# Column sums of a hybrid trunk in two fp32r passes, and low-rank products padded to 128 rows

## The chip, the cores and the metric

One core of one Trainium2 chip runs the whole kernel as one launch. The metric is the device time of that launch in microseconds (us), the median of several runs.

## The reference, cut to what matters

The network is a two-layer trunk on a stream of T = 528 positions (16 meta tokens and 512 inputs) of width 1024. Each layer has a combined input projection, four token mixers (RWKV-7, SSD, retention, RG-LRU), gated merging, an output projection and a SwiGLU block. The change touches sums over channels and the low-rank products of the RWKV mixer:

```
w_log = -softplus(-(w0 + tanh(wd) @ w2)) - 0.5      # rank 64
a = sigmoid(a0 + ad @ a2)                           # rank 64
v = v + (v_first - v) * sigmoid(v0 + (v @ v1) @ v2) # rank 32, second layer only
kk = kk / max(sqrt(sum(kk * kk, head)), 1e-12)      # sum over the 64 channels of a head
var = mean((y - mean)^2, head)
bonus = sum(r * k * r_k, head) * v
y = y * rsqrt(mean(y * y, head) + eps)              # retention, 128 channels
yg = yg * rsqrt(mean(yg * yg, group) + 1e-5)        # SSD, 256 channels
```

## The kernel before

Every activation lies with its channels on the 128 partitions and its 528 positions along the free dimension, as tiles of 128 x 528. A large projection (`dense`, L224 to L238) multiplies eight 128 x 128 weight blocks with eight activation tiles. Weights and activations are split into a high part, rounded to fp32r, and a low part, which is the rest, and three of the four products are taken (high-high, low-high, high-low), each in two halves of 264 columns: 48 matmul instructions on line L236 for one output tile. In the last layer part of the work has 512 columns and then a product is one instruction. The weight split costs one ScalarE copy (L213) and one VectorE subtraction (L214) for each group of eight blocks.

Small products are taken in plain fp32 by `halves` (L258 to L267): for each half of 264 columns it takes a PSUM bank, multiplies, and hands the bank to a function that evicts it. The hardware runs one fp32 product as two matmul instructions, so that the profile counts two for each half. `halves` serves sums over partitions, with a constant matrix as the left side: `ones` (all 128 channels) or `hb` (two blocks of 64 channels). It also serves the low-rank products, whose left side in `sw` and right side (`wdad`, `t32`) use 64 or 32 rows alone: rows 0 to 63 of `wdad` hold the decay's input, rows 64 to 127 that of the in-context rate.

The RWKV mixer works channel block by channel block (8 for each layer). `rwkv_front` (L720) computes keys, decays and the bonus: low-rank products at L736 and L751, the key norm at L756 to L762 (tile `rtmp`), the bonus sum at L790 and L809 (`rtmp` again), and in the second layer the value product at L802 (right side `t32`, called `t` in the profile). `rwkv_inverse` (L813) inverts small triangular blocks, `rwkv_back` (L892) runs the sequential chunks (32 x 32 products at L912 and L918, then a chain over L931, L936 and L947, then the outputs at L964 and L966, squared into `wy` at L975), and `rwkv_finish` (L978) takes the variance sum over `wy` (L981), normalises and multiplies with the gate product `sg` (L986). Retention takes its sum over `rxs` at L479, SSD over two tiles `M` at L654.

What runs between those chains is `others` (L1028): the other three mixers and the merge gates, handed out by `fill` in `layer` in portions of estimated work. The final order of instructions on each engine is not the order of the code: a scheduler sets it when the kernel is built, from its own estimates of durations and from priorities. `soon` raises the priority of evictions. Every engine then runs its own list strictly in order, and waits at an instruction whose input isn't there.

## Time and profile before

| | |
|---|---|
| median of 3 runs | 3588.73 us (3580.23 to 3598.2) |
| the profiled execution's own time | 3595.58 us |
| its span, first to last instruction | 3593.7 us |
| TensorE (PE) busy | 3501.6 us, 97% of the span |
| VectorE (DVE) busy | 2348.2 us, 65% |
| ScalarE (ACT) busy | 1515.9 us, 42% |
| GpSimd (POOL) busy | 175.7 us, 5% |
| mean granted TensorE clock | 0.98 |

PE is the engine for matmuls, PEld its weight loads, which overlap them. Matmuls are pipelined: the duration of one holds its way through the array, and the next one starts long before it ends. What a matmul costs in a full stream is therefore the distance from one end to the next, and not its duration. In a timeline, rows of the same kind that follow one another are merged: the row has the start of the first, the time from there to the end of the last, and their count, so that start plus time is the end of the last. A form such as 64*128 64x264 is a weight tile of 64 rows by 128 columns and a moving tile of 64 rows by 264 columns.

### The profile page before, as it was taken

What the parts mean: (1) busy time and instruction counts of PE and PEld (TensorE: products, weight loads), DVE (VectorE), ACT (ScalarE), POOL (GpSimd) and SP (SyncE); (2) the same over time, 40 slices, a digit from 0 to 9 for tenths busy, and PEclk for the clock granted to TensorE, in tenths of its full rate; (3) what the DMA queues carried; (4) which work ended last, traced back from release to release, by engine and by line L of the source; (5) the groups of instructions that cost most, each with busy time, mean ns of one, the idle gap of its engine ahead of it and who ended that gap; (6) DMA issues with size and microseconds to landing.
All of it is one profiled execution on the core that took longest, in us unless ns stands there. A gap on an engine that the chain in (4) does not pass through costs nothing.

```text
span 3593.7 us, 61305 instructions
## 1 busy us (share of the span) xinstructions
PE 3501.6 (97%) x24768; PEld 3157.5 (88%) x24768; DVE 2348.2 (65%) x4548; ACT 1515.9 (42%) x2208; POOL 175.7 (5%) x474
## 2 busy tenths in 40 slices
PE   8999999999999999999999999899999999999998
PEld 7999889899898999999988888788888887788887
DVE  7787776676787555544347788667668875555543
ACT  6555444434435324222236556344444453332222
POOL 1000100100000000000000000000000000000001
PEclk9999999999999999999999999899999999999999
DMA  3233222222224553233333333222222335533332
GB/s 126 92 100 105 84 81 87 75 83 79 75 87 130 157 171 114 89 94 93 119 103 107 92 97 93 80 87 82 85 77 73 95 117 161 174 116 96 97 95 88
DMA packets 171452, 364.39 MB, mean 101 GB/s; under 512 B 54848, under 2 KB 63424, under 8 KB 171168
## 3 DMA queue, kind: packets, MB, share of 16 engines
q1 hardware_dynamic: 169936, 359.04, 33.0%
q8 instruction: 196, 3.21, 0.4%
q10 hardware_dynamic: 1152, 1.05, 0.1%
q14 instruction: 88, 0.72, 0.1%
q0 software_dynamic: 80, 0.37, 0.0%
HBM read 308.35 MB, written 47.71 MB: 99 GB/s over the span
## 4 chain that ended last, share of the span: by engine, by line
PE 82%; DVE 8%; ACT 6%; DMA 2%; issue 2%; POOL 0%; SPq 0%; DVEq 0%; ACTq 0%; POOLq 0%
PE d L236 63%; PE s L265 4%; PE s L829 2%; PE s L931 1%; DVE wlo L214 1%; PE s L936 1%; PE s L471 1%; PE s L947 1%; PE s L639 1%; PE s L473 1%; ACT whi L213 1%; PE s L395 1%; PE s L632 1%; PE s L918 1%; PE s L912 1%
## 5 line engine op out<-in xcount | busy, mean ns | idle before, releaser
L236 PE MATMUL d<-hh,whi 128*128 128x264 f32 (+1 forms) x4928 | 1196.9, 310 | 18.8 <-ACT whi L213 9.5
L236 PE MATMUL d<-hh,wlo 128*128 128x264 f32 (+1 forms) x4928 | 1188.3, 308 | 0.0
L236 PE MATMUL d<-hl,whi 128*128 128x264 f32 (+1 forms) x4928 | 1187.3, 308 | 0.7 <-DVE hl L255 0.7
L213 ACT ACTIVATE whi<-raw 128x1024 fp32r<-128x1024 f32 (+1 forms) x462 | 485.5, 1051 | 1174.1 <-PE d L236 918.1
L236 PEld LDWEIGHTS d<-hh,whi 128*128 128x128 f32 x4928 | 809.1, 192 | 67.0 <-ACT whi L213 11.2
L236 PEld LDWEIGHTS d<-hl,whi 128*128 128x128 f32 x4928 | 804.6, 191 | 41.8 <-issue 6.4
L236 PEld LDWEIGHTS d<-hh,wlo 128*128 128x128 f32 x4928 | 806.8, 191 | 34.1 <-issue 1.7
L214 DVE TENSOR_TENSOR wlo<-raw,whi 128x1024 fp32r<-128x1024 f32 (+1 forms) x462 | 559.8, 1212 | 342.6 <-ACT whi L213 325.1
L236 PE MATMUL d<-yh,whi 128*128 128x264 f32 (+1 forms) x768 | 206.5, 325 | 4.5 <-ACT yh L254 4.5
L236 PE MATMUL d<-yh,wlo 128*128 128x264 f32 (+1 forms) x768 | 208.1, 324 | 0.0
L236 PE MATMUL d<-yl,whi 128*128 128x264 f32 (+1 forms) x768 | 208.0, 325 | 0.1
L881 DVE TENSOR_TENSOR NS<-NS,sm 36x31 f32<-36x31 f32 (+15 forms) x496 | 164.3, 331 | 11.4
L879 DVE TENSOR_TENSOR sm<-E,NS 36x31 f32<-36x31 f32 (+15 forms) x496 | 164.1, 331 | 11.4 <-DMA E<-xd 0.4
L236 PEld LDWEIGHTS d<-yh,whi 128*128 128x128 f32 x768 | 127.2, 189 | 18.7 <-ACT yh L254 7.9
L236 PEld LDWEIGHTS d<-yl,whi 128*128 128x128 f32 x768 | 128.4, 189 | 12.5 <-DVE yl L255 1.3
L236 PEld LDWEIGHTS d<-yh,wlo 128*128 128x128 f32 x768 | 128.3, 189 | 11.5
L236 PE MATMUL d<-fh,whi 128*128 128x264 f32 (+1 forms) x506 | 132.4, 318 | 0.0
L236 PE MATMUL d<-fl,whi 128*128 128x264 f32 (+1 forms) x506 | 132.0, 317 | 0.0
L236 PE MATMUL d<-fh,wlo 128*128 128x264 f32 (+1 forms) x506 | 131.6, 317 | 0.0
L1141 DVE TENSOR_TENSOR fg<-d,nr 128x528 f32<-128x528 f32 (+1 forms) x44 | 30.8, 700 | 125.7 <-PE d L236 122.4
L1024 DVE SCALAR_TENSOR_TENSOR gth<-gth,d 128x528 f32<-128x528 f32 (+1 forms) x48 | 33.4, 696 | 100.2 <-PE d L236 100.1
L1146 DVE TENSOR_TENSOR fth<-d,fth 128x528 f32<-128x528 f32 (+1 forms) x44 | 30.8, 700 | 92.3 <-PE d L236 92.2
(579 smaller groups left out, 4719.1 us busy)
## 6 DMA issues: line engine op xcount, KB each, us to landing
raw<-w SPq DMA_DIRECT2D x462, 512.0 KB
g<-gth SPq DMA_DIRECT2D x32, 264.0 KB
Bs<-acd SPq DMA_DIRECT2D x32, 264.0 KB
gth<-g SPq DMA_DIRECT2D x32, 264.0 KB
g<-gth SPq DMA_DIRECT2D x32, 256.0 KB
gth<-g SPq DMA_DIRECT2D x32, 256.0 KB
yd<-lt SPq DMA_DIRECT2D x16, 264.0 KB
ya<-wy SPq DMA_DIRECT2D x16, 264.0 KB
```

Source lines behind the costliest of these rows:

```text
L213: nc.scalar.activation(hi[:, :n], raw[:, :n], AF.Copy)
L214: nc.vector.tensor_tensor(out=lo[:, :n], in0=raw[:, :n], in1=hi[:, :n].bitcast(F32), op=SUB)
L236: nc.tensor.matmul(ps[:, h], w[:, k - k0], xv[:, h], start=(k == 0 and w is hi and xi == 0), stop=(k == nk - 1 and w is lo))
L265: self.nc.tensor.matmul(ps, lhsT, rhs[:, o:o + w], start=(i == 0), stop=(i == len(pairs) - 1))
L395: nc.tensor.transpose(ps[:, c * k:c * k + k], src[:, o:o + CL], self.c("ident")[:k, :k])
L471: fs = [lambda: nc.tensor.matmul(o, vTs[e][:, c], scs[e][:, cs], start=(c == 0), stop=True)]
L473: fs.insert(0, lambda: nc.tensor.matmul(o, R[hr, c], qr[hr, cs], start=True, stop=False))
L632: nc.tensor.matmul(ps[:, (c - 3 * a) * CL:(c - 3 * a + 1) * CL], S[:, c, e * 128:e * 128 + 128], Cs[:, c * CL:(c + 1) * CL], start=True, s ...
L639: nc.tensor.matmul(ps[i * 64:i * 64 + 64, (c - 3 * a) * CL:(c - 3 * a + 1) * CL], xdt[:, c, 2 * e + i], Ms[i][:, c * CL:(c + 1) * CL], sta ...
L829: nc.tensor.matmul(ps[:, c - c0], bk[:, c].rearrange("p s x -> p (s x)"), AR[:, c], start=True, stop=True)
L879: nc.vector.tensor_tensor(out=pr, in0=X3[:, :a, a:a + 1].broadcast_to([nl, a, w]), in1=N3[:, a:a + 1, a:].broadcast_to([nl, a, w]), op=MUL)
L881: nc.vector.tensor_tensor(out=N3[:, :a, a:], in0=N3[:, :a, a:], in1=pr, op=ADD)
```

## The change

Sums over partitions go through a new function `sums` in place of `halves`. It copies the input to an fp32r tile `hi` on ScalarE, subtracts that from the input on VectorE into an fp32r tile `lo`, and for each half multiplies both with the constant matrix in fp32r and accumulates them. The constants are loaded once more, as fp32r, into a tile `cr` (index 0 is `ones`, 1 is `hb`), with two transfers issued by GpSimd at the start. `hb` moves to the end of the constants. Four places use it: retention, SSD (two inputs), the key norm and the bonus of RWKV, and its variance. Room for `hi` and `lo` comes from tiles that are not in use there (`v`, `r`, `kkn`, `NS`, `kT`, `rv`, `kr`, `qr`, `z0`, `x0` and so on), which carry their old names in the profile. The tiles `G` and `PS_` of the chunk chain go from two buffers to one. The final norms (`norm_end`, `finish`) and the gate product keep `halves` in fp32.

The low-rank matrices are laid out on the host with zeros: `sw` has three matrices of 128 rows in place of two, the decay's with zeros in rows 64 to 127, the rate's with zeros in rows 0 to 63, and the value's with zeros from row 32. The right sides are then the whole `wdad`, and a `t32` of 128 rows that GpSimd sets to zero once. The transfer of `sw` grows from 128 x 256 to 128 x 384 numbers for each of the 16 channel blocks.

```diff
@@ -122,6 +122,10 @@
         nc.gpsimd.dma_start(out=self.cst, in_=self.io["cst"][:, :NCST0])
+        self.cr = self.t(self.cp, [2, 128], "cr", dt=F32R)
+        for i, name in enumerate(("ones", "hb")):
+            nc.gpsimd.dma_start(out=self.cr[:, i], in_=self.io["cst"][:, COFF[name]:COFF[name] + 128])
         self.kb = self.t(self.cp, 8, "kb")
@@ -265,6 +269,22 @@
                 use(ps, slice(o, o + w))
+    def sums(self, pool, const, xs, use):
+        nc = self.nc
+        parts = []
+        for x, hi, lo in xs:
+            nc.scalar.activation(hi, x, AF.Copy)
+            nc.vector.tensor_tensor(out=lo, in0=x, in1=hi.bitcast(F32), op=SUB)
+            parts += [hi, lo]
+        for o in (0, H2):
+            ps = self.bank(pool)[:, :H2]
+            for i, part in enumerate(parts):
+                nc.tensor.matmul(ps, self.cr[:, const], part[:, o:o + H2], start=(i == 0), stop=(i == len(parts) - 1))
+            with self.soon():
+                use(ps, slice(o, o + H2))
@@ -476,7 +495,9 @@
                     nc.vector.tensor_tensor(out=y[:, ts], in0=ps, in1=gs[e][:, ts], op=MUL)
-            self.halves(self.psm, [(self.c("ones"), sq)], lambda ps, ts: nc.scalar.activation(
+            room = [self.t(p, T, tag, dt=F32R) for tag in ("kr", "qr")] if e else [
+                self.t(p, [NC, 128], "kT", dt=F32R).rearrange("p c x -> p (c x)")[:, :T], self.t(p, T, "rv", bufs=2, dt=F32R)]
+            self.sums(self.psm, 0, [(sq, *room)], lambda ps, ts: nc.scalar.activation(
                 sq[:, ts], ps, AF.Ln, bias=self.bias[1e-6], scale=1.0 / 128))
@@ -649,9 +670,9 @@
             nc.scalar.activation(sq, ys[e], AF.Square)
-            sqs.append((self.c("ones"), sq))
+            sqs.append((sq, self.t(p, T, f"z{e}", dt=F32R), self.t(p, T + 3, f"x{e}", dt=F32R)[:, :T]))
         rs = self.t(p, T, "M", bufs=3)
-        self.halves(self.psm, sqs, lambda ps, ts: nc.scalar.activation(
+        self.sums(self.psm, 0, sqs, lambda ps, ts: nc.scalar.activation(
             rs[:, ts], ps, AF.Ln, bias=self.bias[1e-5], scale=1.0 / 1024))
@@ -713,19 +734,21 @@
                                  stop=(j == NT - 1))
-        self.t32 = self.t(p, T, "t32", bufs=1, parts=32)
+        self.t32 = self.t(p, T, "t32", bufs=1)
+        nc.gpsimd.memset(self.t32, 0.0)
         for h in range(2):
-            nc.scalar.activation(self.t32[:, h * H2:(h + 1) * H2], acc[h], AF.Copy)
+            nc.scalar.activation(self.t32[:32, h * H2:(h + 1) * H2], acc[h], AF.Copy)
     def rwkv_front(self, l, j, p, q):
         nc = self.nc
         m = self.psm
         src = ("w_in", l)
         V = slice(PAD, TP)
-        sw = self.t(p, [2, 128], "sw")
-        nc.sync.dma_start(out=sw, in_=self.io["rsw"][l, j, :, :2])
+        sw = self.t(p, [3, 128], "sw")
+        nc.sync.dma_start(out=sw, in_=self.io["rsw"][l, j, :, :3])
         g2 = self.t(p, 128, "g2", bufs=2)
-        nc.sync.dma_start(out=g2, in_=self.io["rsw"][l, j, :, 2])
+        nc.sync.dma_start(out=g2, in_=self.io["rsw"][l, j, :, 3])
         k = self.shift(self.dense(src, RWKV0 + 1024 + j * 128, self.X), p, "k", 8 + j, PAD)
@@ -748,16 +771,16 @@
         tha = self.t(p, T, "tha")
-        self.halves(m, [(sw[64:128, 0], self.wdad[64:128])], lambda ps, ts: nc.scalar.activation(
+        self.halves(m, [(sw[:, 1], self.wdad)], lambda ps, ts: nc.scalar.activation(
             tha[:, ts], ps, AF.Tanh, bias=self.der("na0", j), scale=-0.5))
         kk = self.t(p, TP, "kkn")
         nc.scalar.activation(kk, k, AF.Copy, scale=self.par("kk", j))
         tmp = self.t(p, T, "rtmp")
         nc.scalar.activation(tmp, kk[:, V], AF.Square)
-        n2 = self.t(p, TP + 1, "r")[:, :T]
-        self.halves(m, [(self.c("hb"), tmp)], lambda ps, ts: nc.vector.tensor_scalar(
-            out=n2[:, ts], in0=ps, scalar1=1e-24, scalar2=None, op0=MAX))
-        nc.scalar.activation(tmp, n2, AF.Ln)
+        room = [self.t(p, TP + 1, tag, dt=F32R)[:, :T] for tag in ("v", "r")]
+        self.sums(m, 1, [(tmp, *room)], lambda ps, ts: nc.vector.tensor_scalar(
+            out=tmp[:, ts], in0=ps, scalar1=1e-24, scalar2=None, op0=MAX))
+        nc.scalar.activation(tmp, tmp, AF.Ln)
         nc.scalar.activation(tmp, tmp, AF.Exp, scale=-0.5)
@@ -799,14 +822,15 @@
             thv = tha
-            self.halves(m, [(sw[0:32, 1], self.t32)], lambda ps, ts: nc.scalar.activation(
+            self.halves(m, [(sw[:, 2], self.t32)], lambda ps, ts: nc.scalar.activation(
                 thv[:, ts], ps, AF.Tanh, bias=self.der("hv0", j), scale=0.5))
             nc.vector.tensor_tensor(out=vd, in0=vd, in1=v[:, V], op=SUB)
             nc.vector.scalar_tensor_tensor(out=vd, in0=thv, scalar=1.0, in1=vd, op0=ADD, op1=MUL)
             nc.vector.scalar_tensor_tensor(out=v[:, V], in0=vd, scalar=0.5, in1=v[:, V], op0=MUL, op1=ADD)
         bv = self.t(q, T, "bv", bufs=2)
         vv = v[:, V]
-        self.halves(m, [(self.c("hb"), tmp)], lambda ps, ts: nc.vector.scalar_tensor_tensor(
+        room = [self.t(p, TP + 1, "r", dt=F32R)[:, :T], self.t(p, TP, "kkn", dt=F32R)[:, :T]]
+        self.sums(m, 1, [(tmp, *room)], lambda ps, ts: nc.vector.scalar_tensor_tensor(
             out=bv[:, ts], in0=ps, scalar=0.5, in1=vv[:, ts], op0=MUL, op1=MUL))
@@ -929,7 +953,7 @@
             nc.tensor.matmul(ps, flat(AR[:, c, 1:3]), flat(SV[:, c]), start=True, stop=True)
-            G = self.t(q, 128, "G", bufs=2)
+            G = self.t(q, 128, "G")
             with self.soon():
@@ -941,7 +965,7 @@
             if c:
-                PS_ = self.t(q, 128, "PS_", bufs=2)
+                PS_ = self.t(q, 128, "PS_")
                 nc.scalar.activation(PS_, flat(SV[:, c]), AF.Copy, scale=Pc)
@@ -975,10 +999,12 @@
-    def rwkv_finish(self, j, back):
+    def rwkv_finish(self, j, back, q):
         nc = self.nc
         y, y2, bv, g2 = back
-        self.halves(self.psr, [(self.c("hb"), y2)], lambda ps, ts: nc.scalar.activation(
+        x = self.t(q, 2 * TP, "NS", dt=F32R)
+        room = x[:, :T], x[:, T:2 * T]
+        self.sums(self.psr, 1, [(y2, *room)], lambda ps, ts: nc.scalar.activation(
             y2[:, ts], ps, AF.Ln, bias=self.bias[64e-5], scale=1.0 / 64))
@@ -1280,11 +1306,11 @@
     s0 = np.concatenate([a["meta"], a["x"][0]], axis=0).T.reshape(NT, 128, T)
-    rsw = np.zeros((DEPTH, NT, 128, 3, 128), np.float32)
+    rsw = np.zeros((DEPTH, NT, 128, 4, 128), np.float32)
     rsw[:, :, :64, 0] = a["rwkv_w2"].reshape(DEPTH, 64, NT, 128).transpose(0, 2, 1, 3)
-    rsw[:, :, 64:, 0] = a["rwkv_a2"].reshape(DEPTH, 64, NT, 128).transpose(0, 2, 1, 3)
-    rsw[:, :, :, 2] = a["rwkv_g2"].reshape(DEPTH, 128, NT, 128).transpose(0, 2, 1, 3)
-    rsw[1:, :, :32, 1] = a["rwkv_v2"].reshape(DEPTH - 1, 32, NT, 128).transpose(0, 2, 1, 3)
+    rsw[:, :, 64:, 1] = a["rwkv_a2"].reshape(DEPTH, 64, NT, 128).transpose(0, 2, 1, 3)
+    rsw[:, :, :, 3] = a["rwkv_g2"].reshape(DEPTH, 128, NT, 128).transpose(0, 2, 1, 3)
+    rsw[1:, :, :32, 2] = a["rwkv_v2"].reshape(DEPTH - 1, 32, NT, 128).transpose(0, 2, 1, 3)
     arrays = {
```

What the change does to the order is seen at three places. In the lists below, rows are PE's or ScalarE's instructions in the order in which the engine runs them; a row with x2 stands for two, and a plain fp32 product is one row though it runs as two instructions.

The first is PE at the end of channel block 0 of layer 0, where `rwkv_finish` takes the variance. Before (`wy` is the squared output, `cst` the constants, `sg` the gate's input):

```order
L236 MATMUL d<-hl,whi 128x264 x2
L236 MATMUL d<-hh,wlo 128x264 x2
L236 MATMUL d<-hh,whi 128x264
L265 MATMUL s<-wy_1495,cst 128x264
L265 MATMUL s<-sg,g_354 128x264
L236 MATMUL d<-hh,whi 128x264
L236 MATMUL d<-hl,whi 128x264 x2
```

After (`NS` holds both halves, `cr` the fp32r constants; L240 is the old L236, L285 the passes of `sums`):

```order
L240 MATMUL d<-hh,whi 128x264
L285 MATMUL s<-NS,cr 128x264 x2
L240 MATMUL d<-hh,whi 128x264
L240 MATMUL d<-hl,whi 128x264 x2
L240 MATMUL d<-hh,wlo 128x264 x2
L240 MATMUL d<-hh,whi 128x264 x2
L240 MATMUL d<-hl,whi 128x264
L285 MATMUL s<-NS,cr 128x264 x2
L240 MATMUL d<-hl,whi 128x264
L240 MATMUL d<-hh,wlo 128x264 x2
```

Before, the second half of the sum stood right ahead of the gate product; now both halves stand a few dense passes apart, each as two fp32r passes, and the gate product follows seven rows behind the last one shown.

The second is PE in channel block 2 of layer 0, where the front of block 3 meets the 32 x 32 products of the back of block 2. Before:

```order
L265 MATMUL s<-wdad,sw 128x264
L912 MATMUL s<-sm,XK 32x32 x9
L918 MATMUL s<-NS,sm 32x32 x9
L265 MATMUL s<-wdad,sw 128x264
L931 MATMUL s<-SV,AR 128x128
L265 MATMUL s<-rtmp,cst 128x264
L918 MATMUL s<-NS,sm 32x32 x9
```

After (L936 and L942 are the old L912 and L918; `v` and `r` are the high and low part of `rtmp`):

```order
L285 MATMUL s<-v,cr 128x264 x2
L240 MATMUL d<-hh,wlo 128x264 x2
L240 MATMUL d<-hh,whi 128x264
L285 MATMUL s<-r,cr 128x264 x2
L240 MATMUL d<-hh,whi 128x264
L936 MATMUL s<-sm,XK 32x32 x9
L240 MATMUL d<-hl,whi 128x264 x2
```

The low-rank products no longer stand among the 32 x 32 products, but as a pair twelve rows ahead of this piece, and the passes of the key norm come ahead of them.

The third is ScalarE in the front of channel block 2 of layer 0, between the low-rank products and the key norm. Before:

```order
L736 ACTIVATE lam<-s,pard 128x264 x2
L754 ACTIVATE kkn<-k,par 128x576
L751 ACTIVATE tha<-s,pard 128x264
L756 ACTIVATE rtmp<-kkn 128x528
L751 ACTIVATE tha<-s,pard 128x264
L760 ACT_TABLE_LOAD
L760 ACTIVATE rtmp<-r 128x528
```

After (L779 is the old L756, L768 and L771 are the old L745 and L748; L279 is the copy to `hi`):

```order
L774 ACTIVATE tha<-s,pard 128x264 x2
L768 ACTIVATE E<-ech 128x9x64
L779 ACTIVATE rtmp<-kkn 128x528
L771 ACTIVATE ech<-ech,kb 128x576
L279 ACTIVATE v<-rtmp 128x528
L217 ACTIVATE whi<-raw 128x1024
```

Two exponentials that stood behind the key norm now stand ahead of its new copy.

## Rows read from the trace of the kernel before

**Rows 1.** Page: span, busy time of each engine, chain that ended last.
```profile
span 3593.7 us, 61305 instructions
PE 3501.6 (97%) x24768; PEld 3157.5 (88%) x24768; DVE 2348.2 (65%) x4548; ACT 1515.9 (42%) x2208; POOL 175.7 (5%) x474
...
PE 82%; DVE 8%; ACT 6%; DMA 2%; issue 2%; POOL 0%; SPq 0%; DVEq 0%; ACTq 0%; POOLq 0%
PE d L236 63%; PE s L265 4%; PE s L829 2%; PE s L931 1%; DVE wlo L214 1%; PE s L936 1%; PE s L471 1%; PE s L947 1%; PE s L639 1%; PE s L473 1%; ACT whi L213 1%; PE s L395 1%; PE s L632 1%; PE s L918 1%; PE s L912 1%
```

**Rows 2.** PE by form: shapes xcount | busy us, mean ns | idle before, releasers.
```profile
L236 PE MATMUL d<-hh,whi 128*128 128x264 f32 x4256 | 923.1, 294 | 18.8 <-ACT whi L213 9.5 <-DVE Cs L313 3.1 <-DVE r L678 2.1
...
L265 PE MATMUL s<-rtmp,cst 128*128 128x264 f32 x128 | 42.5, 436 | 1.7 <-ACT rtmp L756 1.5
L265 PE MATMUL s<-wdad,sw 64*128 64x264 f32 x128 | 41.2, 434 | 0.7 <-ACT lam L736 0.7
...
L265 PE MATMUL s<-rxs,cst 128*128 128x264 f32 x64 | 22.1, 454 | 0.1
L265 PE MATMUL s<-wy,cst 128*128 128x264 f32 x64 | 21.8, 422 | 5.7 <-ACT wy L975 5.2
...
L265 PE MATMUL s<-M,cst 128*128 128x264 f32 x64 | 18.3, 409 | 0.0
...
L265 PE MATMUL s<-t,sw 32*128 32x264 f32 x32 | 9.7, 414 | 0.0
```

**Rows 3.** Timeline of PE around a key norm: start us, us, instructions.
```profile
2086.97 0.41 PE L236 MATMUL d<-hh,whi 128*128 128x264 f32 x2
2087.21 1.05 PE L265 MATMUL s<-rtmp,cst 128*128 128x264 f32 x4
2087.91 0.60 PE L236 MATMUL d<-hl,whi 128*128 128x264 f32 x2
```

**Rows 4.** The same around a low-rank product of 64 rows.
```profile
2080.52 0.40 PE L236 MATMUL d<-hh,wlo 128*128 128x264 f32 x2
2080.86 1.15 PE L265 MATMUL s<-wdad,sw 64*128 64x264 f32 x4
2081.94 0.51 PE L236 MATMUL d<-hh,whi 128*128 128x264 f32 x2
...
2084.69 1.15 PE L265 MATMUL s<-wdad,sw 64*128 64x264 f32 x4
```

**Rows 5.** ScalarE and VectorE by form: the split of a 128 x 528 tile.
```profile
L254 ACT ACTIVATE yh<-yraw 128x528 fp32r<-128x528 f32 x32 | 20.6, 644 | 16.0 <-DMA yraw<-ya 6.6 <-DMA yraw<-yb 4.7 <-DMA yraw<-yc 4.0
...
L255 DVE TENSOR_TENSOR yl<-yraw,yh 128x528 fp32r<-128x528 f32 x32 | 21.5, 703 | 13.5 <-ACT yh L254 13.4
```

**Rows 6.** Line L265: whom PE waited for (us, times).
```profile
its engine sat idle before it (us, times) until:
  ACT wy L975: 14.6, 20
  ACT wy L981: 9.7, 12
...
  ACT rtmp L756: 3.8, 5
```

**Rows 7.** Timeline of a variance sum: ScalarE and the second half on PE.
```profile
412.93 0.62 ACT L975 ACTIVATE wy<-s 64x256 f32<-64x256 f32 x2 [0.49 <-DVE wy L974]
...
414.14 1.28 ACT L981 ACT_TABLE_LOAD   x1
415.44 0.48 ACT L981 ACTIVATE wy<-s,kb 128x264 f32<-128x264 f32 x1
415.94 0.22 ACT L975 ACTIVATE wy<-s 64x64 f32<-64x64 f32 x1
...
416.22 0.71 PE L265 MATMUL s<-wy,cst 128*128 128x264 f32 x2
```

**Rows 8.** Two stretches by window: busy us of each engine, PEclk, DMA share.
```profile
639.00:646.00 7.00, 7.00 (x41) 6.29 (x41) 3.00 (x7) 1.89 (x5) 0.00 (x0) 0.51 0.21 78
902.00:909.00 7.00, 7.00 (x40) 6.08 (x40) 3.63 (x9) 3.42 (x7) 0.34 (x2) 0.52 0.17 68
```

More of the change, by code (lines that the diff above doesn't have):

```diff
@@ L43 @@
     NPAR += _c
-CCOLS = [("ident", 128), ("ones", 128), ("hb", 128), ("cent", 128), ("tri", 128), ("cau", 88),
-         ("qdec", 4 * 88), ("kdec", 4 * 88), ("cdec", 4), ("cos", T), ("sin", T)]
+CCOLS = [("ident", 128), ("ones", 128), ("cent", 128), ("tri", 128), ("cau", 88),
+         ("qdec", 4 * 88), ("kdec", 4 * 88), ("cdec", 4), ("cos", T), ("sin", T), ("hb", 128)]
 COFF, NCST = {}, 0
@@ L56 @@
 GK = 2, 3, 3
-NCST0 = COFF["qdec"]
+NCST0, NCST1 = COFF["qdec"], COFF["hb"]
 def _constants():
@@ L360, in ret_consts @@
     def ret_consts(self, p):
-        n = NCST - NCST0
-        self.rc = self.t(p, n, "rc", bufs=1)
-        self.nc.sync.dma_start(out=self.rc, in_=self.io["cst"][:, NCST0:])
+        self.rc = self.t(p, NCST1 - NCST0, "rc", bufs=1)
+        self.nc.sync.dma_start(out=self.rc, in_=self.io["cst"][:, NCST0:NCST1])
     def rcc(self, name, rows=slice(0, 128)):
@@ L735, in rwkv_front @@
         lv = lam[:, V]
-        self.halves(m, [(sw[0:64, 0], self.wdad[0:64])], lambda ps, ts: nc.scalar.activation(
+        self.halves(m, [(sw[:, 0], self.wdad)], lambda ps, ts: nc.scalar.activation(
             lv[:, ts], ps, AF.Tanh, bias=self.der("hw0", j), scale=0.5))
@@ L1097, in layer @@
                 bk = self.rwkv_back(l, j, fr, iv, p, q)
-                YA.append(self.spill("ya", j, self.rwkv_finish(j, bk)))
+                YA.append(self.spill("ya", j, self.rwkv_finish(j, bk, q)))
                 if j + 1 < NT:
```

## The prediction, made before the changed kernel was run

> **What bounds the kernel now.** I read the page first. PE is busy 97% of a span of 3593.7 us, and the chain that ended last runs over PE for 82%, 63% of it through the dense products of L236 [rows 1]. DVE at 65% and ACT at 42% have room. So the time is, to first order, what PE's list costs when it is run without holes: whatever shortens a PE instruction shortens the kernel, and work added to ACT or DVE costs something where PE's next instruction waits for it. The next view is PE by form [rows 2]. The sums of this change are 128 + 64 + 64 + 64 = 320 instructions, thus 160 fp32 products of 264 columns, and the low-rank products are 128 + 32 instructions, thus 80 products. Their mean durations (409 to 454 ns) say little, since matmuls overlap; what counts is the step from end to end, which I read from the timeline.
>
> The chosen stretch has dense pairs on both sides and no idle time [rows 3]. The dense pair ahead ends at 2086.97 + 0.41 = 2087.38, the four instructions of the key norm at 2087.21 + 1.05 = 2088.26, the next dense pair at 2087.91 + 0.60 = 2088.51. Two fp32 products took 0.88 us, **0.44 each**; two dense fp32r passes took **0.25**. There is no extra step between the two kinds. Around a 64-row product [rows 4] the same reading gives 2080.92, then 2082.01, then 2082.45: the same two products' worth of columns took 1.09 in place of 0.88, and the dense pair behind took 0.44 in place of 0.25. The product is not slower for its columns; the step into the 64-row form and out of it costs 0.21 + 0.19 = **0.40 us a block**, 0.20 a switch.
>
> **The change part by part.**
>
> Sums in fp32r: each of the 160 products becomes two fp32r passes of 264 columns. I price them by the dense pair, because shape, type and a fresh weight load for each pass are the same: 160 x (0.44 - 0.25) = **30.4 us less** on PE. Nearly all of it is on the path, as PE is.
>
> Padding: the low-rank products keep their column count and lose the form of their own. The lists of PE before and after, counted for a change of the rows or columns that neighbouring instructions use, have 607 and 513 such changes. The 94 that go are just the two ends of 47 blocks (37 of `wdad`, 10 of `t`) in the list before. 94 x 0.20 = **18.8 us less**. The 32-row blocks of `t` are priced as the 64-row ones, since their mean duration is alike (414 and 434 ns) [rows 2]. The new zero rows cost nothing on PE: the full-row product costs 0.44.
>
> One rule speaks against padding. In the rows, the decay's and the rate's products of a channel block stand 3.8 us apart with dense passes between [rows 4], so nothing of one runs beside the other. The Trainium skill, "TensorE: Matmul & The Clock Gate", section "Why this matters for your kernels", says that products of few rows that lie in distinct row groups run concurrently, so padding would give that up; by it, 16 pairs of blocks could overlap, and 16 x 0.88 = 14 us of room would be lost. The two blocks aren't neighbours in PE's list before, so the sum takes nothing for it.
>
> The new step ahead of each sum: a copy on ACT (0.644 us) and a subtraction on DVE (0.703) for a 128 x 528 tile [rows 5], 80 of each. That is 52 us for ACT and 56 for DVE, which go to about 44% and 68%. As load it lies beside PE; as latency it puts 1.35 us ahead of 72 sums (16 key norms, 16 bonuses, 16 variances, 16 in retention, 8 in SSD). What that costs depends on how far the scheduler moved the sums back in PE's list. I counted PE's rows between the last instruction that feeds a sum and the sum, at prices of the trace. Variance: median 0.85 us before, 2.8 after, so 1.9 gained against 1.35. Here the rows hold a possible gain too. PE waited 14.6 us for `wy` and 9.7 for the bank that L981 frees [rows 6], and the second half came late because a table load and the first half's logarithm (1.28 + 0.48) ran ahead of the last square [rows 7]; with the copy reading the whole tile they can't come between. I take 0, between 24 less and 16 x 1.35 = 22 more. Bonus: the passes stand 13 or more dense passes later (1.6 us) in 14 of 16 blocks, so 0. Retention: the first half can't start before the second half's square now, but the median distance grows from 1.7 to 2.9, so 0 to 2. SSD: 0, at most 8 x 1.35 = 11. Key norm: the distance grows by only 0.7 of the 1.35, and in some blocks one or two exponentials stand ahead of the copy on ACT; 16 x 0.65 = 10, of which I let 2 vanish in slack (PE waited just 3.8 there) [rows 6]. The value for all is **8 us more**, with ends at 24 less and 72 x 1.35 = 97 more; I stay near the lower end because the order shows the sums moved by more than their new step in three of five kinds.
>
> What hangs on the moved instructions: behind a waiting sum stand the dense passes, and PE can't pass it. On ACT the copy delays the next weight copy `whi` by 0.64, on DVE the subtraction delays `wlo` by 0.70; both run a group ahead of PE. Behind the variance's wait stands the gate product, which used to wait for a bank in any case.
>
> The rest I cost at nothing. Two transfers for `cr` and a memset for `t32` go to GpSimd, at 5% busy [rows 1], long before their first use. The queue of `sw` carries 64 KB more for each of 16 blocks, issued a block ahead. `G` and `PS_` with one buffer: their next writer depends, through the chain, on their last reader anyway. The list of ACT has 174 table loads in place of 190, 16 x 1.28 = 20 us of ACT, off the path. If GpSimd's transfers were late, the first key norm (at some 37 us) would wait a few us, once.
>
> Sum: -30.4 - 18.8 + 8 = -41.2. The profiled execution took 3595.58 us, so 3554.4; it lies 6.9 above the median of the runs (3588.73), so on the median's scale **3548 us**, 1.1% less.
>
> **The rivals.**
>
> *The new step becomes the wait.* PE stands at each sum until ACT and DVE have split its input. For it: the order of ACT shows exponentials and `whi` copies ahead of the new copy in places, and PE's waits at L265 for ACT show that the scheduler already placed these sums too early [rows 6]. Against: it pushed them back this time. The gains of 49.2 us are used up at 0.68 us a sum over 72 sums. Over 0.93 us a sum it is slower by more than 0.5%; all 97 give 3589 - 49 + 97 = 3637. Between 0.43 and 0.93 it comes out at 3571 to 3607, which is no difference (0.5%, some 18 us, is about what a measurement of this kernel can tell from none).
>
> *Padding gives nothing*, because another form of the 32 x 32 or 88-row products sits beside the block anyway or the switch hid other waits: 3548 + 19 = 3567.
>
> *The fp32r sums don't run at the dense pace*, since the second pass waits for the low part that is 0.7 us behind the high one, or small groups cost more than long runs: half of the 30 goes, 3563.
>
> *The clock.* In two stretches where the front's small products stood among 32 x 32 products, the granted clock was 0.51 and 0.52, thus 1.2 GHz for nearly all of 7 us, while PE was counted busy throughout [rows 8]. Each cost some 3.5 us, and the mean of 0.98 over 3593.7 us is some 72 us of full pace withheld in all. In the new order these products stand among dense passes. If five such stretches ran at 2.4 GHz, that is 17 us more gained: 3531; if the reshuffled list made as many new ones, 3565.
>
> **How the numbers follow.** Forecast 0.60, by itself 3530 to 3566; clock much better 0.10 (about 3525); padding without effect 0.07; fp32r at half its gain 0.04; waits that eat most of the gain 0.13; waits that make it slower 0.06. So faster by over 0.5% (below 3571) is 0.81, the same 0.13, slower 0.06. The range 3522 to 3584 leaves out the slower case, the upper half of the middle one and the far end of the clock's, some 0.17.
>
> **What would show it.** In the changed profile the passes of `sums` should be 320 with means like the dense ones (some 290 ns), and step 0.12 to 0.13 from end to end. `wdad` blocks of four should take 0.88 and the dense pair behind 0.25. PE's idle time ahead of the sums should be near 20 to 35 us in all, mostly at the key norm with DVE as releaser; over 70 there proves the first rival. ACT should gain some 30 us in all (52 less 20 of table loads) and DVE 56. If PE's busy time falls by 50 and the span by far less, the forecast's waits were wrong; if the `wdad` blocks still step 1.09, the padding's term was.

## The result, and the profile of the changed kernel

The changed kernel took **3562.4 us** (median of 4 runs, 3550.0 to 3565.2) beside 3589.6 for the kernel before in the same comparison: ratio 0.9924, 95% interval 0.9901 to 0.9947. That is 27 us or 0.8% less. It was forecast to be 3548, 41 us less, so the time lies inside the range, and a third of the gain is missing. The profiled execution took 3565.2 us (span 3563.4).

The page of the changed kernel, span and busy time by engine, answers [rows 1]: PE lost 44.8 us of busy time, VectorE gained 47.9 and ScalarE 26.6, and PE stayed at 97%.

```profile
span 3563.4 us, 61528 instructions
...
PE 3456.8 (97%) x24768; PEld 3141.3 (88%) x24768; DVE 2396.1 (67%) x4628; ACT 1542.5 (43%) x2272; POOL 185.6 (5%) x477
```

PE by form answers [rows 2] (columns as there): the passes of the sums have means of 326 to 328 ns beside 293 of the dense ones (290 were forecast), and the padded blocks are cheaper (396 ns for 434, 388 for 414).

```profile
L240 PE MATMUL d<-hh,whi 128*128 128x264 f32 x4256 | 913.8, 293 | 23.1 <-ACT whi L217 9.6 <-DVE Cs L333 6.5 <-DVE r L699 2.0
...
L269 PE MATMUL s<-wdad,sw 128*128 128x264 f32 x128 | 35.8, 396 | 1.9 <-ACT lam L759 1.9
...
L285 PE MATMUL s<-r,cr 128*128 128x264 f32 x64 | 15.8, 328 | 1.7 <-DVE r L280 1.7
L285 PE MATMUL s<-NS,cr 128*128 128x264 f32 x64 | 15.7, 327 | 1.7 <-ACT NS L279 1.1 <-DVE NS L280 0.3
L269 PE MATMUL s<-t,sw 128*128 128x264 f32 x32 | 9.0, 388 | 0.0
...
L285 PE MATMUL s<-v,cr 128*128 128x264 f32 x32 | 7.8, 326 | 6.0 <-ACT v L279 5.9
```

PE's timeline around a key norm of the changed kernel answers [rows 3]. The high parts of both halves are one pair (`v`), the low parts another (`r`), and dense passes go between.

```profile
2443.78 0.41 PE L240 MATMUL d<-hh,whi 128*128 128x264 f32 x2
2444.02 0.41 PE L285 MATMUL s<-r,cr 128*128 128x264 f32 x2
2444.26 0.41 PE L240 MATMUL d<-hl,whi 128*128 128x264 f32 x2
```

The pairs end at 2444.19, 2444.43 and 2444.67: 0.24 us for two passes of the sum, as for two dense ones. PE's timeline around a low-rank block answers [rows 4]:

```profile
235.95 0.41 PE L240 MATMUL d<-hh,wlo 128*128 128x264 f32 x2
236.20 1.05 PE L269 MATMUL s<-wdad,sw 128*128 128x264 f32 x4
236.89 0.60 PE L240 MATMUL d<-hh,whi 128*128 128x264 f32 x2
```

The block of four steps from 236.36 to 237.25, 0.89 us, and the dense pair behind it to 237.49, 0.24. The forecast had 0.88 and 0.25.

What the sums wait for, all of line L285 (engine and line, us, times), answers [rows 6]:

```profile
its engine sat idle before it (us, times) until:
  ACT v L279: 14.1, 16
  ACT NS L279: 5.0, 15
  DVE r L280: 4.5, 8
```

That is some 26 us with the small entries, inside the 20 to 35 forecast, mostly at the key norm, though ScalarE's copy releases it and not VectorE. This view counts the idle time of the weight loads too, and most of it lies under passes that still run: by form (above) PE itself stood only 6.0 + 1.7 + 1.7 us there, against 5.7 + 1.7 in the kernel before [rows 2]: 2 us more where 8 were forecast. The same holds for [rows 6]: where it has 14.6 and 9.7 us, PE itself stood 5.7 us at `wy` [rows 2] and 3.4 at the gate product.

```profile
L265 PE MATMUL s<-sg,g 128*128 128x264 f32 x64 | 20.2, 404 | 3.4 <-ACT wy L981 3.3
```

The largest loss stands elsewhere, in PE's timeline of the second layer:

```profile
2203.32 0.40 PE L240 MATMUL d<-hh,wlo 128*128 128x264 f32 x2
2215.14 1.17 PE L936 MATMUL s<-sm,XK 32*32 32x32 f32 x18 [11.42 <-DVE ends L542]
...
2228.51 0.79 PE L240 MATMUL d<-hh,whi 128*128 128x264 f32 x2
```

The first 32 x 32 product behind the block's inverse waits 11.42 us, and no dense pass runs until 2228.51. It reads the transposes of L927 shown below, which end at 2215.09; the profile names `ends`, a copy right behind them. The windows of that stretch (busy us of PE, PEld, DVE, ACT and POOL, then PEclk, the granted clock, DMA share, GB/s):

```profile
2203.00:2215.00 12.00, 0.73 (x7) 0.52 (x5) 11.91 (x20) 3.80 (x4) 5.37 (x9) 0.63 0.45 120
2215.00:2228.00 13.00, 9.45 (x98) 8.10 (x98) 8.17 (x21) 1.54 (x3) 1.71 (x2) 0.50 0.07 20
```

While PE stands, VectorE is busy 11.91 of 12 us; then PE runs at 1.2 GHz, and ScalarE does almost nothing. VectorE's and ScalarE's timelines say with what:

```profile
2198.46 3.43 DVE L193 RECIPROCAL dtd<-dtd 16x528 f32<-16x528 f32 x1
...
2214.65 0.44 DVE L927 STREAM_TRANSPOSE sm<-NS 32x288 f32<-32x288 f32 x1
```

```profile
2224.23 0.64 ACT L279 ACTIVATE r<-rtmp 128x528 fp32r<-128x528 f32 x1 [16.85 <-DVE v L829]
2224.96 0.40 ACT L969 ACTIVATE PS__24184<-SV,Pc 128x128 f32<-128x128 f32 x1
2225.27 0.59 ACT L393 ACTIVATE rx<-d 128x528 f32<-128x528 f32 x1
```

VectorE does the SSM stage's softplus among the last steps of the inverse, and so is late with the transpose that PE wants. And ScalarE stands 16.85 us at the bonus sum's copy: its room `r` still holds the value residual in the second layer. Behind the copy waits the eviction that frees a bank for dense passes.

**Two measures** for what follows. A run's span times its granted clock is taken as what the run would take at full clock. For one kernel its standard deviation from run to run is 2 to 3 us and that of the time 4 to 8: the kernel before gave 3523.9 to 3525.6 as means of four comparisons (74 runs), whose medians went from 3584 to 3593. The rest of the span is what the clock took. The kernel before lost 57.7 to 66.0 us that way in the four comparisons, so the clock is compared within one comparison only. The other measure adds up each PE instruction's step from end to end in a trace, with time at 1.2 GHz counted half, and apart from it PE's idle time (with some 9.5 us ahead of its first instruction) and that half; some 9 us behind its last instruction complete the span:

```
profiled trace          PE's work   idle   clock
before                     3435.7   83.3    66.0
padding alone              3425.1   89.6    57.6
padding and split step     3419.5   84.8    61.3
fp32r sums alone           3401.5   90.1    61.0
changed kernel             3390.4   97.5    66.4
```

There is one trace for each kernel, so differences of a few us are weak. And the two measures can't be added up: span times clock books half of any idle time at 1.2 GHz as the clock's, while the traces keep it as idle time. That half is 4.0, 3.8, 5.2, 10.7 and 10.4 us in these five traces, from top to bottom.

### The profile page after: what moved, and what is told of

Same layout as the page of the kernel before. It is cut to its first block, busy times and chain, and to the rows that moved or that the text cites. A ratio compares the mean times of both kernels' runs of the same rounds, so it can differ in the third digit from the quotient of the medians.

```text
span 3563.4 us, 61528 instructions
## 1 busy us (share of the span) xinstructions
PE 3456.8 (97%) x24768; PEld 3141.3 (88%) x24768; DVE 2396.1 (67%) x4628; ACT 1542.5 (43%) x2272; POOL 185.6 (5%) x477
## 5 line engine op out<-in xcount | busy, mean ns | idle before, releaser
L240 PE MATMUL d<-hh,whi 128*128 128x264 f32 (+1 forms) x4928 | 1189.0, 309 | 23.8 <-ACT whi L217 9.6
L240 PE MATMUL d<-hl,whi 128*128 128x264 f32 (+1 forms) x4928 | 1188.6, 308 | 1.1 <-DVE hl L259 1.0
L240 PE MATMUL d<-hh,wlo 128*128 128x264 f32 (+1 forms) x4928 | 1180.5, 307 | 0.7 <-DVE wlo L218 0.6
L240 PEld LDWEIGHTS d<-hh,whi 128*128 128x128 f32 x4928 | 808.5, 192 | 64.0 <-ACT whi L217 9.6
L240 PEld LDWEIGHTS d<-hl,whi 128*128 128x128 f32 x4928 | 807.3, 191 | 35.7 <-DVE hl L259 2.3
L240 PEld LDWEIGHTS d<-hh,wlo 128*128 128x128 f32 x4928 | 805.5, 191 | 33.2 <-issue 2.2
L240 PE MATMUL d<-yh,whi 128*128 128x264 f32 (+1 forms) x768 | 206.0, 324 | 5.1 <-ACT yh L258 5.1
L240 PE MATMUL d<-yl,whi 128*128 128x264 f32 (+1 forms) x768 | 208.0, 324 | 0.5 <-DVE yl L259 0.5
L240 PE MATMUL d<-yh,wlo 128*128 128x264 f32 (+1 forms) x768 | 206.7, 323 | 0.0
L240 PEld LDWEIGHTS d<-yh,whi 128*128 128x128 f32 x768 | 126.6, 188 | 19.7 <-ACT yh L258 9.1
L240 PEld LDWEIGHTS d<-yl,whi 128*128 128x128 f32 x768 | 127.9, 188 | 13.4 <-DVE yl L259 2.0
L240 PEld LDWEIGHTS d<-yh,wlo 128*128 128x128 f32 x768 | 127.6, 188 | 11.0
L240 PE MATMUL d<-fh,whi 128*128 128x264 f32 (+1 forms) x506 | 132.3, 318 | 0.0
L240 PE MATMUL d<-fl,whi 128*128 128x264 f32 (+1 forms) x506 | 132.0, 317 | 0.0
L240 PE MATMUL d<-fh,wlo 128*128 128x264 f32 (+1 forms) x506 | 131.5, 316 | 0.0
```

Source lines behind the costliest of these rows:

```text
L240: nc.tensor.matmul(ps[:, h], w[:, k - k0], xv[:, h], start=(k == 0 and w is hi and xi == 0), stop=(k == nk - 1 and w is lo))
```

## Experiments

All runs, in us; "clock" is what the clock took, with what it took of the kernel before in the same comparison. For the changed kernel's own comparison that second value isn't recorded; from its times it is about 63.

```
                         median   ratio to before (95%)    at full clock   clock (before)
changed kernel           3562.4   0.9924 (0.9901-0.9947)      3481.7        76.5 (63)
padding alone            3588.8   1.0003 (0.9988-1.0018)      3515.6        70.2 (59.7)
fp32r sums alone         3562.3   0.9935 (0.9910-0.9961)      3487.5        73.0 (59.7)
other room               3561.3   0.9930 (0.9907-0.9953)      3486.5        71.8 (59.7)
transposes ahead         3562.2   0.9938 (0.9917-0.9960)      3489.5        71.8 (59.7)
before, 47/34            3599.3   1.0020 (1.0004-1.0035)      3520.6        75.8 (66.0)
before, 49/32            3600.1   1.0031 (1.0014-1.0049)      3537.5        62.1 (66.0)
changed, 47/34           3560.8   0.9922 (0.9895-0.9948)      3487.9        71.2 (66.0)
changed, 49/32           3570.1   0.9942 (0.9924-0.9961)      3491.5        77.0 (66.0)
softplus earlier         3561.8   0.9928 (0.9909-0.9947)      3485.5        72.4 (57.7)
SSM sums in fp32         3557.2   0.9921 (0.9906-0.9936)      3487.7        66.3 (57.7)
both of these            3556.9   0.9914 (0.9898-0.9931)      3488.4        64.6 (57.7)
split step, fp32 product 3576.7   0.9970 (0.9953-0.9987)      3505.1        70.0 (61.6)
```

**The padding alone**, in the kernel before:

```diff
-        self.halves(m, [(sw[0:64, 0], self.wdad[0:64])], lambda ps, ts: nc.scalar.activation(
+        self.halves(m, [(sw[:, 0], self.wdad)], lambda ps, ts: nc.scalar.activation(
...
-            self.halves(m, [(sw[0:32, 1], self.t32)], lambda ps, ts: nc.scalar.activation(
+            self.halves(m, [(sw[:, 2], self.t32)], lambda ps, ts: nc.scalar.activation(
```

> The kernel before with the padding alone: the low-rank products take 128 rows, every sum stays one fp32 product. My theory prices 94 changes of form at 0.20 us: 18.8 us less than the kernel before, thus about 3571, with PE's work at full pace (its span less idle time and less half of the half-clock time) lower by 19 and the blocks of four wdad products stepping 0.88 with 0.25 for the dense pair behind. Rival, padding gives nothing by itself because the switch hid waits: within 5 us of the kernel before, with the work lower and the idle time higher by as much.

It came out at 1.0003: no change in the time. The lists of PE, VectorE and ScalarE are instruction for instruction those of the kernel before, so nothing but the form differs on these engines. A block and the pair behind it in its timeline:

```profile
2068.25 0.41 PE L236 MATMUL d<-hh,wlo 128*128 128x264 f32 x2
2068.49 1.05 PE L265 MATMUL s<-wdad,sw 128*128 128x264 f32 x4
2069.19 0.60 PE L236 MATMUL d<-hh,whi 128*128 128x264 f32 x2
```

Ends at 2068.66, 2069.54 and 2069.79: 0.88 and 0.25, as forecast. Yet PE's work fell by 10.6 us and not 18.8. Changes of form, counted with rows and columns taken as 32, 64 or 128, fall from 607 to 525, by 82 and not 94: some ends of the 47 blocks stand beside another form, and the rest of the 94 went with the new order. Counted over the trace of before, only 31 of the 47 blocks have a dense pass next behind them; there the first pass fell from 0.32 to 0.15 us (5.3 in all). What stands behind the other 16, other small products, gave back 1.4 us in all. Inside the blocks 7.1 us went and not 9.4, and other passes cost some 3 more. And of the 10.6, idle time took back 6.3: PE is earlier at places where others are late. The key norm in this trace:

```profile
L265 PE MATMUL s<-rtmp,cst 128*128 128x264 f32 x128 | 38.8, 404 | 3.9 <-ACT rtmp L757 3.8
```

against 1.7 [rows 2]. In the traces 4 us remain; in the runs 9.4 at full clock, and the clock took 10.5 us more than of the kernel before.

**The sums alone**: the same hunks the other way round, in the changed kernel.

> The changed kernel with the low-rank products on 64 and 32 rows again, the sums still in two fp32r passes. My theory: PE's work at full pace 30 us lower than in the kernel before, idle time ahead of the sums not higher, so 3590 - 30 = about 3560 if the planner's list is no worse, 3567 with the 8 us of waits that the prediction took. Rival, the split step is what ate the missing gain: 3575 or more, with PE's idle time ahead of the sums 15 us or more above the kernel before.

3562.3: all of the change's gain comes with the sums and their list. PE's work is 34.2 us below that of the kernel before, its idle time 6.8 above. The lists are in turn those of the changed kernel, so the two are a second pair that differs by the padding alone: PE's work 11.1 lower with it, idle time 7.4 higher, the time the same (3562.3 and 3562.4).

**The step without its gain**, in the changed kernel:

```diff
-            nc.vector.tensor_tensor(out=lo, in0=x, in1=hi.bitcast(F32), op=SUB)
-            parts += [hi, lo]
+            nc.vector.tensor_tensor(out=lo.bitcast(F32), in0=x, in1=hi.bitcast(F32), op=MAX)
+            parts += [lo.bitcast(F32)]
...
-                nc.tensor.matmul(ps, self.cr[:, const], part[:, o:o + H2], start=(i == 0), stop=(i == len(parts) - 1))
+                nc.tensor.matmul(ps, self.cr[:, const].bitcast(F32), part[:, o:o + H2], start=(i == 0), stop=(i == len(parts) - 1))
```

> The changed kernel with the new step but without its gain: ScalarE copies and VectorE works on the same tiles as the split does (the larger of the input and its rounded copy, which is the input), and PE then takes one fp32 product per half, as before. Against the run with the padding alone (span times granted clock 3515.6) this is the price of the step by itself. The prediction's term, 8 us of added waits: 3520 to 3528. Rival, the split step becomes the wait, 0.68 us or more at each of 72 sums: 3550 or more. And no price at all, since the planner moves the sums back by itself: within 3 of 3515.6. What the clock takes tells more: in the eight lists with fp32r sums it is 5 to 15 us above the kernel before in the same call. If the shorter PE work is the cause, here it is within 5 us; if the other order is, it is again 5 to 15 us above.

None of the three: it is 10.5 us *lower* at full clock than the padding alone (9.6 with each against the kernel before of its own comparison), and 3576.7 in time. VectorE and ScalarE do all the added work, page:

```profile
PE 3480.8 (97%) x24768; PEld 3155.8 (88%) x24768; DVE 2397.3 (67%) x4628; ACT 1549.1 (43%) x2276; POOL 182.5 (5%) x477
```

and PE still does fp32 products. With a step ahead of each sum the planner makes another list, and PE's idle time and work cost 4.8 and 5.6 us less than with the padding alone. That isn't because the sums wait less: by form PE's idle time ahead of them is about 2 us higher, and the largest fall, 7.6 us, is ahead of the products with `AR` and `bk` (L829 before). So the price of the new step, together with the rooms and single buffers that this run has too, is below nothing, which the prediction's lower end (24 less, from the waits at the variance) allowed and its value (8 more) did not. In the changed kernel PE stood 1.7 us at the variance sums (`NS` above), 5.7 before (`wy`) [rows 2]. From here to the changed kernel only fp32r is added, under a new list: PE's work falls by 29.1 (forecast 30.4), and idle time rises by 12.7, of which 11.4 is the one wait at 2215. The clock took 8.4 us more than of the kernel before, but that says little, since the padding that this run holds brings the same 70 us by itself.

**What makes the wait at 2215.** Two runs, one for each of the engines shown above:

```diff
-        room = [self.t(p, TP + 1, "r", dt=F32R)[:, :T], self.t(p, TP, "kkn", dt=F32R)[:, :T]]
+        hi = self.t(p, TP, "ech", dt=F32R) if l else self.t(p, TP + 1, "r", dt=F32R)
+        room = [hi[:, :T], self.t(p, TP, "kkn", dt=F32R)[:, :T]]
```

> The changed kernel, but in the second layer the high half of the bonus sum goes into the tile of the decay's running sum (ech), not into the tile that holds the value residual there (r). Theory one: the copy into r stood 16.85 us on ScalarE behind the residual's last step on VectorE, held the evictions and weight copies queued behind it, and so took PE's dense passes away at 2203 to 2233; without that conflict the copies in the second layer wait under 3 us each, that place loses under 5 us, and the time falls by 15 to 25 us to 3538 to 3547. Rival: the stretch at 2203 comes from where the planner put VectorE's work (the softplus ahead of the block's transposes); then the wait of PE for these transposes stays near 11 us and the time stays within 8 us of 3562.

```diff
-            nc.vector.transpose(NTr[b0], N[b0, :, h, :32])
+            with self.soon():
+                nc.vector.transpose(NTr[b0], N[b0, :, h, :32])
```

> The changed kernel with one priority more: the 32 transposes of the inverse on VectorE, for which PE waited 11.42 us at 2215, are put ahead like the evictions are. Theory of VectorE's list: that wait falls under 3 us and with it the half-clock stretch behind it (27 us long), so 3562 falls by 11 to 25 us. Rival, the room conflict on ScalarE: the wait is shorter, but ScalarE still stands over 10 us for the residual in the second layer and the time stays within 8 us of 3562.

Neither changed the time. In the first, ScalarE's copy waits 4.6 us in place of 16.85, but ScalarE then stands 12.5 us at its next copy, of the chunk chain, and PE's longest wait behind its first instruction (us, times, longest) only moved to the bonus sum:

```profile
PE s L285 <- ACT ech L279: 10.3, 2, 8.9
```

since the copy into `ech` must wait for VectorE's products, which stand behind the softplus too. In the second PE waits 11.4 us as before: the transposes need the inverse back from its transfers, which the changed kernel's trace has issued at 2210.7 to 2212.1, so priority at the end of that chain is no cure. And the room on ScalarE was not the cause: without the conflict no dense pass runs for 23.6 us at this place, with it for 24.8.

**The list with the same work.** Two numbers share the dense work out over a channel block:

```diff
-F1, F2, F3 = 48.0, 33.0, 170.0
+F1, F2, F3 = 47.0, 34.0, 170.0
```

> The kernel before, whose work is the same to the last instruction's size, in another list: the two planner's numbers that share the dense work out over a channel block go from 48 and 33 to 47 and 34. In the runs so far, span times granted clock is 3525 for the kernel before and what the clock takes is 60 us of its span; in the four kernels with parts of the change it takes 70 to 77. Theory one, the list: the order of before happens to lose little, and any other list loses 70 or more, so this one takes 3596 or more at a product of 3525. Theory two, the work: with fewer PE cycles among the small products the clock is granted less often, which this kernel doesn't touch: 60 us lost and 3583 to 3592.

> The same as the run with 47 and 34, in the other direction: 49 and 32 in the kernel before. Theory one, the list: 70 us or more lost to the clock, 3596 or more. Theory two, the work: 60 us lost and 3583 to 3592.

> The changed kernel with 47 and 34 in place of 48 and 33. Span times granted clock 3480 to 3490 by both theories, since the work is that of the changed kernel. Theory one, the list: what the clock takes scatters from list to list, 60 to 80 us, as it would in the kernel before, so 3545 to 3570. Theory two, the work: 70 to 77 us lost again, 3556 to 3566.

> The changed kernel with 49 and 32. Theory one, the list: a product of 3480 to 3490 and 60 to 80 us lost to the clock, 3545 to 3570. Theory two, the work: 70 to 77 us lost, 3556 to 3566.

Before was the best of its three lists, by 0.2 and 0.3%, once through the clock (75.8 against 66.0) and once through the time at full clock (3537.5). So where a list puts the same work moves the time by 7 to 11 us, up to a quarter of what was forecast. The forecast for "other list" held for the one and not for the other, whose clock loss was 62. Of the changed kernel one list is as fast (3560.8) and one 9 us slower than that one. Both theories are too simple.

**Softplus and SSM sums.** The softplus in the second layer was written two LRU blocks earlier, the SSM sums set back to fp32, and both:

```diff
+            if j == (5 if l else 7):
+                yield from self.ssm_common(l, X)
...
-            sqs.append((sq, self.t(p, T, f"z{e}", dt=F32R), self.t(p, T + 3, f"x{e}", dt=F32R)[:, :T]))
+            sqs.append((self.c("ones"), sq))
```

> The changed kernel with the SSM stage's common part (a softplus over 16 rows, 8.5 us on VectorE with its reciprocal of 3.4) written after the sixth LRU block of the second layer and not after the eighth. In every list with fp32r sums so far the softplus stands some 22 rows ahead of the inverse's transposes on VectorE in that layer, and PE stood 9 to 11.4 us there; in the lists of the kernel before it stands 43 to 47 rows behind them, and PE didn't stand there. In this list it stands some 60 rows behind. Theory one, the placement: the long wait and the 24 to 27 us at half clock behind it go, span times granted clock falls from 3482 to 3470 to 3476, and the time from 3562 to 3540 to 3552. Rival, VectorE is short of time in this stage wherever the softplus stands: a wait of similar size shows up at another product, the time stays within 6 us of 3562.

> The changed kernel with the SSM stage's eight sums as fp32 products again (no copy, no subtraction there). In the traces so far the stage of the second layer lost 8 to 17 us to the clock and 10.5 to 12.6 us of idle time in the six lists with fp32r sums, and 3 to 7 and 8 to 11 us in the four without. Theory one, the split step in the stage: both fall back to the lower values there, 7 and 3 us less, against 6 us more of PE's work for 32 products, so the time is 3555 to 3563. Rival, the stage only stands beside the change: its losses stay, the time goes up by the 6 us of work to 3565 to 3570.

> The two edits together: the SSM stage's sums in fp32 and the softplus after the sixth LRU block of the second layer. If both theories hold, 3535 to 3550, the fastest so far; if only the placement counts, 6 us above the run with the placement alone; if neither, 3562 to 3572.

With the softplus earlier the 11 us wait is gone and nothing is won. The windows of the same place in that trace (columns as above):

```profile
2193.00:2207.00 14.00, 11.72 (x79) 9.48 (x77) 8.99 (x21) 4.53 (x8) 1.32 (x2) 0.52 0.17 53
2210.00:2231.00 21.00, 14.22 (x49) 11.21 (x50) 9.69 (x29) 5.85 (x10) 0.00 (x0) 0.51 0.21 69
```

By its timeline no dense pass runs from 2194.8 to 2225.4; PE goes through the steps of the block's state recursion, one after the other at 1.2 GHz, with 0.3 to 0.8 us of idle time at most of them. The rival's time holds (3561.8) but not its reason: no wait of similar size shows up there, and VectorE is busy 18.7 of the 35 us. What remains is the place itself, where the LRU blocks end and retention begins: PE's list has too little dense work there. It has in the kernel before, for a shorter time:

```profile
2243.00:2256.00 13.00, 6.80 (x38) 5.07 (x37) 12.00 (x21) 1.86 (x3) 0.00 (x0) 0.78 0.08 18
```

The wait at 2215 was one shape of that hole and not its cause. The fourteen traces fall into two groups there: no dense pass runs there for 15.1 to 17.6 us in the five lists with fp32 sums, the one with the split step and an fp32 product among them, and for 23.6 to 30.9 us in the nine with fp32r sums. So the longer hole goes with the fp32r sums and not with the step ahead of them or the padding; by which wait the list comes to it is not shown. It was 16.3 us in the kernel before, 24.8 in the changed one and 30.6 with the softplus earlier; the clock withheld 5.1, 11.2 and 13.6 us of them.

The SSM sums in fp32 come out at a ratio of 0.9921, both edits together at 0.9914, against 0.9924; the intervals overlap, so no version here is shown to be faster than the changed kernel. The clock took 9 and 7 us more than of before, less than in most other changed lists, and in the second layer's stage it took 10 and 8 us, against 8 to 17 in the seven traces with fp32r sums there and 12 in the one with the step and an fp32 product. That is in the direction of the theory, and not enough to show it.

## Why the prediction was right, and where it was off

- **What bounds the kernel** held in the main: PE's list. But the sum took that list to run without new holes, and it did not: PE's idle time rose by 14.2 us in the traces, 8.6 of them at one place of the second layer that no term covers (the hole between the LRU blocks and retention).
- **The sum** came out near at full clock, 43 us for 41.2, and that is luck. Taken one after the other, the padding, the step and fp32r are worth some 9, 10 and 24 us there, where 18.8 less, 8 more and 30.4 less were forecast: the step's error covers the other two.
- **fp32r passes** (-30.4): right as work, -29.1, by passes of 0.12 us. Of that 12.7 us came back as idle time, 11.4 of it in one wait.
- **Padding** (-18.8): mis-sized. The prices of [rows 3, 4] were right where a dense pass stands behind, and I took them for all 47 blocks; only 82 of the 94 changes go with the padding, and they aren't worth 0.20 us each. Work fell by 10.6 and 11.1, idle time took back 6.3 and 7.4, and the time fell by nothing, in two pairs with equal lists. The rival "padding gives nothing" is what happened, in part by the ways that it named (another form beside the block, hidden waits) and in part through the clock, which it did not name.
- **Added waits** (+8): wrong in sign for the step. The new list with the step was some 10 us shorter at full clock, 12 in time. "The new split step becomes the wait" is refuted as a price of the step. The term's lower end, 24 less, rests on 14.6 and 9.7 us of [rows 6] that were not all waits of PE. As the idle time of the whole change the term was too low: in the traces PE's busy time fell by 44.8 us and the span by 30.3, which the prediction named as its sign of wrong waits; the idle time stands mostly at other products than the sums.
- **Other room and rest at nothing**: no run speaks against it, though single buffers and transfers were not tested by themselves. The bonus copy into `r` holds ScalarE for 16.85 us in the second layer; with other room the time was the same.
- **The clock** (0) is the other term put at nothing. At full clock the change is worth 3525 - 3481.7 = 43 us. The clock took some 13 us more, which leaves the 27 to 29 that the medians and the means show. This is the side of the clock rival priced at 3565 ("the reshuffled list made as many new ones"). But not all of the 13 is PE at work on a slower clock: half of the idle time at 1.2 GHz, 10.4 us against 4.0 in the traces, is in it. What PE's own work lost there is nearly equal, 66.4 and 66.0, though the trace of before is of a run with a low clock (0.980). So about half of the 13 us is the new idle time. That the rest comes from the list alone isn't so: the padding alone lost 10.5 more in the very list of the kernel before.
- **Against padding** the prediction weighed a rule of the Trainium skill, "TensorE: Matmul & The Clock Gate", section "Why this matters for your kernels": products of few rows in distinct row groups run concurrently. It did not come into play here: in both pairs PE's work was lower with 128 rows.

**What stays open** is why the clock takes 5 to 15 us more in each list with the fp32r sums, beyond the half of the idle time at 1.2 GHz (6.2 to 11.9 us in these nine traces, 3.1 to 5.2 in the other five), and 10 more for the padding, where that half is equal. Less PE work in the same chain of small products, and thus an emptier PE, would fit the padding; another list would fit the run with 47/34. The runs don't tell them apart.

## What to carry to other kernels

Price a cheaper instruction by its neighbours in the list, block by block, not by a count of form changes; and ask of each place whether PE, once early there, finds more than a wait. Under a planner, an added step with slack can lead to a better list, so a step's price needs a run that has the step without its gain. Span times granted clock is steadier than the time, but it books half of the idle time at 1.2 GHz as the clock's: read idle time from the trace beside it. Where the order was tuned for the kernel before, take several lists of the same work before a difference of 0.3% is put down to a change.

## What the runs showed of the hardware

- The kernel before took 3573 to 3610 us in its runs, with a standard deviation of 5 to 8 us within a comparison, and 2 to 3 for span times granted clock: nearly all the scatter is the clock's. Comparing at full clock told terms of 10 us apart that the times alone left within their intervals.
- The same instructions in the same order, 47 blocks of them in a cheaper form, ran at a granted clock of 0.980 in place of 0.983 (12 and 17 runs), which gave all of the gain back.
- With the softplus earlier, the clock was at 1.2 GHz through 34 of the 35 us in the two windows at the recursion's steps, while PE counted as busy 26 of them.
